# Three blocks of the input projection cut anew, the first one changing from eight products to seven on its way

## The chip, the cores and the metric

The kernel runs on one core of a Trainium2 chip. The metric is the device time of one execution in microseconds (us); smaller is better. A core has TensorE (matrix products), VectorE, ScalarE and GpSimd (element-wise work), and SyncE, whose queue issues all transfers of this kernel. In the profile they are PE (PEld for the loading of weights), DVE, ACT, POOL and SP.

## The reference: what is computed

One layer of a streaming encoder runs for 2048 prompt tokens and 32 sample tokens, which share the weights. The model width is 1024. Only the first step matters here, the combined input projection of the normed tokens:

```python
hp = rmsnorm(xp, g_pre_mix[l])
qa, ka, va, qb, kb, vb, g_low, r = jnp.split(h @ w_in, IN_OFFSETS, axis=-1)
```

`w_in` has 1024 rows and 3088 columns: queries, keys and values of a banded softmax attention (512 columns each), queries and keys (256 each) and values (512) of a gated linear attention (GLA), 16 columns for a forget gate of low rank, and 512 columns `r` for an output gate. Behind it come both attentions, an output projection, cross-attention into 256 memory rows, and a SwiGLU feed-forward of hidden width 2816.

All is in float32, and the kernel gets float32 accuracy out of a faster matmul type: every operand is split into a high part and a low part, and each product is made of three matmuls (high x high, high x low, low x high).

## The kernel before

**Pairs and blocks.** The 2080 tokens are cut into three blocks (`PB`, L604) of 256, 384 and 400 token pairs. A block of h pairs holds 2h neighbouring tokens; its first h tokens are column half c = 0, the other h are c = 1. The 1024 rows of the contraction are halved too (kh = 0 and 1, four tiles of 128 rows each). So the product of a block with 256 columns of `w_in`, which are themselves two halves of 128, is a product of two 2x2 block matrices.

**Eight or seven products.** Multiplied plainly, such a product takes eight half-size products (`fm_eight` L868, and `eight` inside `tm_unit` L920). Block 0 is done so: its moving operands are x times the gain, without the norm, which is multiplied in when a result leaves the accumulator (`r0`, L724). Blocks 1 and 2 use a scheme of the Strassen-Winograd kind with seven products (`fm_unit` L888, `seven` inside `tm_unit`): `seven_mov` (L663) forms sums and differences of the four quarters of x in place and splits seven operands, `seven_sta` (L678) does the same to the weights, and results are combined when they are evicted. With seven products, the norm has to be multiplied into x first (`scale`, L777).

**Units.** A block is worked through in ten units, in this order: a (attention values and the 16 gate columns, token-major, 264 columns to a matmul), two units of queries, two of keys, one of GLA queries, one of GLA keys, two of gates, and v (GLA values, token-major, 256 columns). The eight units between a and v are feature-major: their matmuls have as many columns as the block has pairs. A feature-major unit takes 96 matmuls by eight products and 84 by seven; a token-major one takes 96 or 84 for each 128 tokens of a column half. The last block has 16 tokens over in each half, its tail, with 48 matmuls more in each token-major unit.

**What VectorE does in it.** For a seven-product unit it makes four sums or differences and seven low parts of 512 elements per partition (twice as many of 264 or 256 columns in the token-major units), three of the seven evictions, and for queries and keys two more low parts of the results. For an eight-product unit there are four low parts and no sums. Between blocks it makes the moving operands: four sums and seven low parts of 4h elements. ScalarE makes the high parts.

**Buffers.** The seven moving operands have a buffer each (`mps`, L709); block 0 puts its four operands into the first four (`first_operands`, L808). Seven "stage" buffers (L710) hold raw x, squares and results on their way out; eight buffers hold split weights, four hold raw ones, four hold results that wait to be combined (`cp`). The accumulators have three banks for X, three for Y and Z, and two for small things.

**Order.** Within the program, loads and norms of the next block are woven between the units of the present one (`weave`, L598). The true order of each engine's queue is then made by a planner (`Order`, L49 to 487): it holds a cost for every instruction, plays the whole kernel forward and backward many times with priorities that are partly drawn at random, and fixes the best order it met. Each engine's queue runs in the order fixed there, SyncE's transfers among them. So a change at one place can reorder other places.

**Behind the projection.** Results go to DRAM in pieces by block (`PBLK`, L605) and are read back by the attentions, which begin near 530 us. They cut the tokens by another table (`BLK`).

Of the kernel before, what the change touches and what calls it, by code (L numbers as in the profile page):

```python
# [11 lines left out]
F32R = mybir.dt.float32r  # L12
AF = mybir.ActivationFunctionType
ALU = mybir.AluOpType
# [5 lines left out]
P = 128  # L20
# [4 lines left out]
T = TP + TS  # L25
# [465 lines left out]
def encoder_step(ctx, tc, ins, outs):  # L491
# [27 lines left out]
    gains = {}  # L519
# [81 lines left out]
        return [it for *_, it in sorted(todo, key=lambda x: x[:3])]  # L601


    PB = [(0, 256), (512, 384), (1280, 400)]  # L604
    PBLK = [(s, 2 * h) for s, h in PB]  # L605
    BLK = [(0, 512), (512, 512), (1024, 512), (1536, 544)]
    NB = len(BLK)
# [46 lines left out]
    HK = KT // 2  # L654
# [50 lines left out]
    with ExitStack() as ph:  # L705
        def pool(name, bufs, **kw):
            return ph.enter_context(tc.tile_pool(name=name, bufs=bufs, **RW, **kw))

        mps = [pool(f"pm{i}", 1) for i in range(7)]  # L709
        stp = pool("pst", 7)  # L710
        wp = pool("pw", 8)
        cpp = pool("pc", 4)
# [13 lines left out]
        def stage(name, dt=F32):  # L726
            return stp.tile([P, 1600], dt, tag="stage", name=name)


        def quarters(b, first=False):  # L730

            s, h = PB[b]
            raw, rst = {}, {}

            def load(c, kh):
                r = stage(f"x{b}_{kh}{c}")[:, : HK * h].rearrange("p (k n) -> p k n", k=HK)
                raw[kh, c] = r
                with tc.high_priority(offset=2 * PRI if first else 0):
                    SP.dma_start(r, xt_in[kh * 512 : kh * 512 + 512, s + c * h : s + c * h + h].rearrange("(k p) n -> p k n", p=P))

            def squares(c, kh):
                if first:
                    sq = stage(f"xs{b}_{c}{kh}")[:, : HK * h].rearrange("p (k n) -> p k n", k=HK)
                    ACT.activation(sq, raw[kh, c], AF.Square)
                    add(DVE, sq[:, 0:2], sq[:, 0:2], sq[:, 2:4])
                    if kh == 0:
                        rst["sq", c] = sq
                        return
                    add(DVE, sq[:, 0:2], sq[:, 0:2], rst["sq", c][:, 0:2])
                    rst["sq", c] = sq  # L750
                    return
                if kh == 0:
                    rst[c] = nrm.tile([P, 400], F32, tag="rs", name=f"xr{b}_{c}")[:, :h]
                for kk in range(HK):
                    if kh == 0 and kk == 0:
                        ACT.activation(rst[c], raw[kh, c][:, kk], AF.Square)
                    else:
                        sq = nrm.tile([P, 400], F32, tag="sq", name=f"xs{b}_{c}{kh}{kk}")[:, :h]
                        ACT.activation(sq, raw[kh, c][:, kk], AF.Square)
                        add(POOL, rst[c], rst[c], sq)  # L760

            def rstd(c):
                ps = pt.tile([P, 512], F32, tag="pt", name=f"xn{b}_{c}")
                if first:
                    nt = h // P
                    for kk in range(2):
                        PE.matmul(ps[:, :h], lhsT=ones, rhs=rst["sq", c][:, kk], start=kk == 0, stop=kk == 1)
                    for t in range(nt):
                        for kk in range(2):
                            PE.matmul(ps[:, h + t : h + t + 1], lhsT=rst["sq", c][:, kk, t * P : t * P + P], rhs=ones[:, 0:1], start=kk == 0, stop=kk == 1, skip_group_check=True)  # L770
                    ACT.activation(ps[:, : h + nt], ps[:, : h + nt], AF.Ln, bias=eps_t, scale=1.0 / D)
                    ACT.activation(r0[:, c, : h + nt], ps[:, : h + nt], AF.Exp, scale=-0.5)
                    return
                PE.matmul(ps[:, :h], lhsT=ones, rhs=rst[c], start=True, stop=True)
                rst[c] = rstd_of(ps[:, :h], D)

            def scale(c, kh):  # L777
                for kk in range(HK):
                    v = raw[kh, c][:, kk]
                    DVE.scalar_tensor_tensor(out=v, in0=v, scalar=gains["g_pre_mix"][:, kh * HK + kk : kh * HK + kk + 1], in1=rst[c], op0=ALU.mult, op1=ALU.mult)  # L780

            items = []
            for c in range(2):
                items += [partial(load, c, 0), partial(load, c, 1)]
            for c in range(2):
                items += [partial(squares, c, 0), partial(squares, c, 1), partial(rstd, c)]
                if not first:
                    items += [partial(scale, c, 0), partial(scale, c, 1)]
            return items, raw

        def operands(b, raw):
            h = PB[b][1]
            ops, tail = [], None
            if b == len(PB) - 1:
                tail = kp.tile([P, 2, KT, 32], F32R, tag="tail", name="tail")
                for (kh, c), r in raw.items():
                    t = tail[:, :, kh * HK : kh * HK + HK, c * 16 : c * 16 + 16]
                    split(t[:, 0], t[:, 1], r[:, :, h - 16 : h], DVE)

            def put(v, eng):  # L800
                m_ = mps[len(ops)].tile([P, 2, HK, 400], F32R, tag="mov", name=f"mi{b}_{len(ops)}")
                split(m_[:, 0, :, :h], m_[:, 1, :, :h], v, eng)
                ops.append((m_[:, 0, :, :h], m_[:, 1, :, :h]))

            seven_mov(raw, put)
            return ops, tail
# [80 lines left out]

        def fm_unit(b, ops, col, name):  # L888

            if b == 0:  # L890
                return fm_eight(b, ops, col, name)
            h = PB[b][1]
            w = weights_fm(col, name)
            st = stage(name + "_st")[:, : 4 * h].rearrange("p (a n) -> p a n", a=2)
            dst = {(a, c): st[:, a, c * h : c * h + h] for a in range(2) for c in range(2)}
            cp = [cpp.tile([P, 800], F32, tag="cp", name=f"{name}_c{i}")[:, :h] for i in range(3)]

            def prod(ps, i, first):
                mm3(ps, [((w[i][0][:, k], w[i][1][:, k]), (ops[i][0][:, k], ops[i][1][:, k])) for k in range(HK)], first, True, not first)

            X = px.tile([P, 512], F32, tag="px", name=name + "_X")[:, :h]
            Y = py.tile([P, 512], F32, tag="py", name=name + "_Y")[:, :h]
            Z = py.tile([P, 512], F32, tag="py", name=name + "_Z")[:, :h]
            prod(X, 0, True)
            out(ACT.copy, cp[0], X)
            prod(Y, 1, True)
            out(ACT.copy, cp[1], Y)
            prod(X, 2, False)
            out(ACT.copy, cp[2], X)
            prod(Y, 3, False)  # L910
            out(add, DVE, dst[0, 1], cp[2], Y)
            prod(X, 4, False)
            out(add, DVE, dst[1, 1], cp[1], X)
            prod(Z, 5, True)
            out(add, DVE, dst[0, 0], cp[0], Z)
            prod(X, 6, False)
            out(ACT.copy, dst[1, 0], X)
            return st

        def tm_unit(b, ops, tail, col, low, dst, name):  # L920
# [66 lines left out]
                        for a in range(2):  # L987
                            out(ACT.mul, st[c][:, t, a], banks[a][t], r0[:, c, h + t : h + t + 1])

            T = seven() if b else eight()  # L990
            lt = kp.tile([16, 800], F32, tag="lt", name=name + "_low") if low else None

            def gate(view, n, t0):
# [118 lines left out]

            return [partial(load, 0), partial(load, 1), partial(squares, 0), partial(squares, 1), scale]

        items, raw = quarters(0, True)
        with tc.high_priority(offset=2 * PRI):
            for it, by in zip(items, (0.0, 0.0, 3000.0, 3000.0, 6000.0, 6000.0, 6000.0, 6000.0 + 3000.0, 6000.0 + 3000.0, 6000.0 + 3000.0)):
                with issue_order.shifted(by):
                    it()
        for b in range(len(PB)):  # L1120
            ops, tail = operands(b, raw) if b else first_operands(raw)
            units = [partial(tm_unit, b, ops, tail, 1024, True, vad[b], f"wva{b}")]
            units += [partial(queries, b, ops, u) for u in range(2)] + [partial(keys, b, ops, u) for u in range(2)]
            units += [partial(gla_qk, b, ops, 1536, qbd, 0.125, f"wqb{b}"), partial(gla_qk, b, ops, 1792, kbd, None, f"wkb{b}")]
            units += [partial(gates, b, ops, u) for u in range(2)]
            units += [partial(tm_unit, b, ops, tail, 2048, False, vbd[b], f"wvb{b}")]
            if b == 0:
                units = [units[i] for i in FIRST_ORDER]
            extra = []
            if b == 0:  # L1130
                extra += [partial(load_gain, g) for g in ("g_post_mix", "g_pre_mem", "g_mem", "g_post_mem", "g_pre_ffn", "g_post_ffn")]
            if b == 1:
                extra += [bias_rows] + [partial(bias_copies, h) for h in range(HA)]
            if b + 1 < len(PB):
                items, raw = quarters(b + 1)
                extra += items
            else:
                extra += mem_norm()
            for it in units[:1] + weave(units[1:-1], extra) + units[-1:]:
                it()  # L1140
        SP.dma_start(outs["av_t"], vad[-1][256:])


    DVE.tensor_scalar(out=g16, in0=gains["g_pre_mem"], scalar1=0.0625, scalar2=None, op0=ALU.mult)
# [689 lines left out]
    with ExitStack() as ph:  # L1834
# [255 lines left out]
        late = []  # L2090
# [680 lines left out]
```

## Time and profile before

| What | us |
|---|---|
| Median of three runs | 2903.05 (2900.72 to 2905.3) |
| The profiled execution | 2903.03 |
| Its span in the profile | 2901.2 |
| First matmul of the projection | 7.88 |
| Block 0's last unit ends, block 1 begins | 151.70 |
| Block 1's last unit ends, block 2 begins | 333.9 |
| The projection's last matmuls, memory keys begin | 529.83 |

A row of a group of instructions names the line, the engine, the operation, what is written and read, the shape, the count, then the busy time and the mean duration in ns of one, then the idle time of the engine just before them and what ended it. A line is often that of a helper: L596 is every matmul of the projection and L529 every low part, so tiles are told apart by name: `wva` is a, `wqa`, `wka`, `wqb`, `wkb` and `wr` are queries, keys, GLA queries, GLA keys and gates, `wvb` is v, `mi` a moving operand; `_s` is a split weight, `_st` a result, `_c` one that waits to be combined. A timeline row has the start, the length, and how many instructions were merged into it.

### The profile page before, as it was taken

How to read it: one execution, taken by the hardware profiler on the slowest of the kernel's cores; microseconds unless marked ns; L12 is line 12 of the kernel's file. 1: busy time of each engine (PE TensorE's matmuls, PEld its weight loads, DVE VectorE, ACT ScalarE, POOL GpSimd, SP SyncE). 2: the span in 40 equal slices, each digit the busy share in tenths (PEclk: the TensorE clock that was granted, in tenths of full speed). 3: DMA queues.
4: the chain of work that ended last, by engine and by line, in shares of the span. 5: the costliest groups of instructions: out<-in, count | busy, mean ns of one | idle time of the engine just before them, and what ended most of it. 6: DMA issues, size and time to landing. Idle time of an engine off the chain costs nothing.

```text
span 2901.2 us, 49346 instructions
## 1 busy us (share of the span) xinstructions
PE 2856.5 (98%) x18162; PEld 2442.1 (84%) x18162; DVE 1888.6 (65%) x3366; ACT 1497.7 (52%) x2996; POOL 649.6 (22%) x982
## 2 busy tenths in 40 slices
PE   8999999999999999999999999999999999999998
PEld 8999999887888787987888888887888878777888
DVE  5687976576675667785578766657655556345655
ACT  5556655567786777676546533335433334323333
POOL 0202000367585757000003111113111111000013
PEclk9999999999999999999999999999999999999999
DMA  7656374786586757557567555455543345886665
GB/s 207 198 169 209 118 214 143 240 256 197 175 272 183 230 168 232 176 173 238 185 218 240 181 176 171 151 171 201 168 157 104 119 145 174 284 287 224 204 228 187
DMA packets 463862, 563.90 MB, mean 194 GB/s; under 512 B 55777, under 2 KB 309802, under 8 KB 463586
## 3 DMA queue, kind: packets, MB, share of 16 engines
q1 hardware_dynamic: 463618, 560.73, 60.1%
q8 instruction: 143, 2.34, 0.3%
q14 instruction: 101, 0.83, 0.1%
HBM read 399.75 MB, written 164.02 MB: 194 GB/s over the span
## 4 chain that ended last, share of the span: by engine, by line
PE 58%; DMA 1%; POOL 0%; ACT 0%; DVE 0%; issue 0%; DVEq 0%; ACTq 0%; POOLq 0%
PE pdn L596 13%; PE pg_X L596 8%; PE pu_X L596 8%; PE mops L596 6%; PE pg_Y L596 4%; PE pu_Y L596 4%; PE ms_X L596 3%; PE pg_Z L596 2%; PE pu_Z L596 2%; PE wops L596 2%; PE ms_Y L596 2%; PE ms_Z L596 1%; PE mpt L2007 0%; PE tsgate L2383 0%; PE tsup L2383 0%; PE utp L2592 0%
## 5 line engine op out<-in xcount | busy, mean ns | idle before, releaser
L596 PE MATMUL pdn<-ur,wd_s 128*128 128x512 f32 (+1 forms) x1980 | 431.1, 378 | 4.5 <-ACT ur L533 3.4
L596 PEld LDWEIGHTS pdn<-ur,wd_s 128*128 128x128 f32 x1980 | 354.6, 188 | 77.9 <-ACT ur L533 4.2
L596 PE MATMUL pg_X<-mf,wg_s 128*128 128x512 f32 x1056 | 262.2, 393 | 0.0
L596 PE MATMUL pu_X<-mf,wu_s 128*128 128x512 f32 x1056 | 258.8, 390 | 0.0
L596 PEld LDWEIGHTS pg_X<-mf,wg_s 128*128 128x128 f32 x1056 | 197.4, 188 | 47.4 <-issue 6.0
L596 PEld LDWEIGHTS pu_X<-mf,wu_s 128*128 128x128 f32 x1056 | 198.3, 188 | 42.1
L529 DVE TENSOR_TENSOR wu_s<-wu_r,wu_s 128x512 fp32r<-128x512 f32 x154 | 107.7, 702 | 145.8 <-ACT wu_s L528 141.9
L528 ACT CAST wg_s<-wg_r 128x512 fp32r<-128x512 f32 x154 | 95.4, 621 | 172.9 <-PE pu_X L596 70.5
L596 PE MATMUL mops<-mo,vw 128*128 128x512 f32 x768 | 180.7, 394 | 0.0
L529 DVE TENSOR_TENSOR wg_s<-wg_r,wg_s 128x512 fp32r<-128x512 f32 x154 | 111.7, 727 | 99.3 <-ACT wg_s L528 98.1
L596 PEld LDWEIGHTS mops<-mo,vw 128*128 128x128 f32 x768 | 143.5, 188 | 32.7 <-issue 1.9
L528 ACT CAST wu_s<-wu_r 128x512 fp32r<-128x512 f32 x154 | 95.2, 621 | 142.9 <-PE pg_X L596 51.4
L1570 PE MATMUL wops<-om,wo_s 128*128 128x512 f32 x576 | 154.3, 405 | 1.3 <-POOL om L534 1.0
L534 DVE TENSOR_TENSOR ur<-ur 128x2048 fp32r<-128x2048 f32 (+1 forms) x42 | 90.4, 2154 | 65.2 <-ACT ur L533 65.2
L596 PE MATMUL pg_Y<-mf,wg_s 128*128 128x512 f32 x528 | 130.0, 391 | 0.0
L596 PE MATMUL pu_Y<-mf,wu_s 128*128 128x512 f32 x528 | 129.9, 391 | 0.0
L534 POOL TENSOR_TENSOR mf<-mf 128x512 fp32r<-128x512 f32 x24 | 39.2, 1661 | 402.8 <-DMA hop<-hp 382.1
L1570 PEld LDWEIGHTS wops<-om,wo_s 128*128 128x128 f32 x576 | 104.1, 188 | 24.0 <-POOL om L534 1.7
L533 ACT CAST ur<-ur 128x2048 fp32r<-128x2048 f32 (+1 forms) x42 | 74.1, 1765 | 96.6 <-DMA ur<-ud 96.3
L596 PEld LDWEIGHTS pu_Y<-mf,wu_s 128*128 128x128 f32 x528 | 99.1, 188 | 21.5
L596 PEld LDWEIGHTS pg_Y<-mf,wg_s 128*128 128x128 f32 x528 | 99.0, 188 | 21.4
L1249 PE MATMUL s<-ks,qbuf 128*128 128x256 f32 (+2 forms) x448 | 112.7, 342 | 4.3 <-DVE u_mn L1224 3.9
(606 smaller groups left out, 6535.1 us busy)
## 6 DMA issues: line engine op xcount, KB each, us to landing
ud<-u SPq DMA_DIRECT2D x154, 256.0 KB, 3.8
ur<-ud SPq DMA_DIRECT2D x28, 1024.0 KB, 6.7
wg_r<-in_w_ffn_gate_dram SPq DMA_DIRECT2D x44, 512.0 KB, 3.8
wu_r<-in_w_ffn_up_dram SPq DMA_DIRECT2D x44, 512.0 KB, 5.5
wd<-in_w_dn_dram SPq DMA_DIRECT2D x72, 256.0 KB, 4.7
wo_r<-in_w_o_dram SPq DMA_DIRECT2D x64, 256.0 KB, 3.9
mf<-hop SPq DMA_DIRECT2D x14, 1024.0 KB, 7.4
wdr<-in_w_dn_dram SPq DMA_DIRECT2D x22, 512.0 KB, 6.2
```

The costliest lines, as they stand in the source:

```text
L528: ACT.copy(hi, src)
L529: (lo_eng or DVE).tensor_tensor(out=lo, in0=src, in1=hi.bitcast(F32), op=ALU.subtract)
L533: ACT.copy(m[:, 0], m[:, 1].bitcast(F32))
L534: (POOL if on_pool else DVE).tensor_tensor(out=m[:, 1], in0=m[:, 1].bitcast(F32), in1=m[:, 0].bitcast(F32), op=ALU.subtract)
L596: PE.matmul(ps, lhsT=a, rhs=b, start=first and i == 0, stop=last and i == len(seq) - 1, skip_group_check=skip)
L1249: PE.matmul(ps_out, lhsT=q[:, 2 * i + e, q0 : q0 + nq], rhs=ks[:, e, k0 : k0 + ncol], start=i == 0, stop=i == 1)
L1570: PE.matmul(ps, lhsT=a, rhs=b, start=i == 0, stop=i == len(seq) - 1)
```

## The change

The blocks become 384, 384 and 272 pairs. Block 0 begins with eight products as before, but only for its first three units (a and both query units, `EIGHT = 3`). Then a step `late` multiplies gain and norm into the raw x of block 0, which is kept until then, and makes the seven operands; keys, GLA, gates and v of block 0 go by seven products. The seven operands of every block get their buffers in another order (`HOME`), so that the first three don't lie in those that the eight products read. Block 2, now the narrowest, goes by seven products as before.

```diff
-    PB = [(0, 256), (512, 384), (1280, 400)]
+    PB = [(0, 384), (768, 384), (1536, 272)]
...
-        mps = [pool(f"pm{i}", 1) for i in range(7)]
+        HOME = (4, 5, 6, 0, 1, 2, 3)
+        mps = {i: pool(f"pm{i}", 1) for i in HOME}
...
+        EIGHT = 3
...
             def scale(c, kh):
+                r = r0[:, c, :h] if first else rst[c]
                 for kk in range(HK):
                     v = raw[kh, c][:, kk]
-                    DVE.scalar_tensor_tensor(out=v, in0=v, scalar=gains["g_pre_mix"][:, kh * HK + kk : kh * HK + kk + 1], in1=rst[c], op0=ALU.mult, op1=ALU.mult)
+                    DVE.scalar_tensor_tensor(out=v, in0=v, scalar=gains["g_pre_mix"][:, kh * HK + kk : kh * HK + kk + 1], in1=r, op0=ALU.mult, op1=ALU.mult)
...
-                m_ = mps[len(ops)].tile([P, 2, HK, 400], F32R, tag="mov", name=f"mi{b}_{len(ops)}")
+                m_ = mps[HOME[len(ops)]].tile([P, 2, HK, 400], F32R, tag="mov", name=f"mi{b}_{len(ops)}")
...
-            if b == 0:
+            if type(ops) is dict:
                 return fm_eight(b, ops, col, name)
...
-            T = seven() if b else eight()
+            T = eight() if type(ops) is dict else seven()
...
+            def late():
+                nonlocal ops
+                for it in scales:
+                    it()
+                ops, _ = operands(0, raw0)
...
             if b == 0:
                 units = [units[i] for i in FIRST_ORDER]
+                raw0 = raw
+                units[EIGHT - 1 : EIGHT] = [units[EIGHT - 1], late]
...
-        SP.dma_start(outs["av_t"], vad[-1][256:])
+        SP.dma_start(outs["av_t"], vad[-1][PBLK[-1][1] - 544 :])
```

The last line only follows the new cut: the same rows are copied out.

More of the change, by code (lines that the diff above doesn't have):

```diff
@@ L788, in quarters @@
                     items += [partial(scale, c, 0), partial(scale, c, 1)]
-            return items, raw
+            return items, raw, [partial(scale, c, kh) for c in range(2) for kh in range(2)]
         def operands(b, raw):
@@ L1113, in mem_norm @@
             return [partial(load, 0), partial(load, 1), partial(squares, 0), partial(squares, 1), scale]
-        items, raw = quarters(0, True)
+        items, raw, scales = quarters(0, True)
         with tc.high_priority(offset=2 * PRI):
@@ L1120, in encoder_step, with unit @@
         for b in range(len(PB)):
[L1121 to L1126, printed above, removed]
+            if b == 0:
+                ops, tail = first_operands(raw)
+            else:
+                ops, tail = operands(b, raw)
+            def unit(f, *a):
+                return lambda: f(a[0], ops, *a[1:])
+            def late():
[3 more added lines that the diff above has]
+                ops, _ = operands(0, raw0)
+            units = [unit(tm_unit, b, tail, 1024, True, vad[b], f"wva{b}")]
+            units += [unit(queries, b, u) for u in range(2)] + [unit(keys, b, u) for u in range(2)]
+            units += [unit(gla_qk, b, 1536, qbd, 0.125, f"wqb{b}"), unit(gla_qk, b, 1792, kbd, None, f"wkb{b}")]
+            units += [unit(gates, b, u) for u in range(2)]
+            units += [unit(tm_unit, b, tail, 2048, False, vbd[b], f"wvb{b}")]
             if b == 0:
                 units = [units[i] for i in FIRST_ORDER]
+                raw0 = raw
+                units[EIGHT - 1 : EIGHT] = [units[EIGHT - 1], late]
             extra = []
@@ L1134, in encoder_step @@
             if b + 1 < len(PB):
-                items, raw = quarters(b + 1)
+                items, raw, _ = quarters(b + 1)
                 extra += items
```

## The prediction

> **What bounds the kernel now.** I read the page first (shares and slices), then the table of stretches cut at the units of the projection, TensorE's timeline for the price of one matmul of each width, VectorE's groups by form, and the list of TensorE's waits.
>
> ```profile
> span 2901.2 us, 49346 instructions
> PE 2856.5 (98%) x18162; PEld 2442.1 (84%) x18162; DVE 1888.6 (65%) x3366; ACT 1497.7 (52%) x2996; POOL 649.6 (22%) x982
> PE wva_X L596 <- ACT wva_s L528: 7.9, 1, 7.9
> PE wqa_X L596 <- ACT wqa_c L700: 1.7, 1, 1.7
> ```
>
> TensorE is busy for 98% of the span. In the projection (0 to 530 us) it waits twice: 7.9 us before the first matmul and 1.7 us in the first query unit of block 1. So a microsecond of matmuls taken out is a microsecond of time, as long as the other engines keep up. VectorE is the next engine: it prepares the moving operands, the weights and a part of the evictions. The table of stretches gives length, then TensorE, weight loads, VectorE, ScalarE, GpSimd busy, clock, DMA share and GB/s. A stretch is one or two units: v of block 0; a of block 1; first queries of block 1; v of block 1; a of block 2; then queries, keys, the two GLA units and gates of block 2.
>
> ```profile
> 129.00:151.70 22.70, 22.70 (x195) 22.70 (x194) 18.15 (x20) 14.65 (x21) 0.00 (x0) 1.00 0.32 103
> 151.70:182.30 30.60, 30.60 (x255) 30.58 (x254) 26.73 (x41) 16.39 (x31) 0.00 (x0) 1.00 0.38 123
> 182.30:212.00 29.70, 27.98 (x162) 27.27 (x161) 20.32 (x31) 14.86 (x31) 0.00 (x0) 1.00 0.78 233
> 304.05:333.90 29.85, 29.85 (x253) 29.85 (x253) 26.54 (x39) 22.14 (x36) 0.00 (x0) 1.00 0.38 126
> 333.90:370.50 36.60, 36.60 (x306) 35.92 (x304) 31.59 (x44) 18.23 (x37) 0.00 (x0) 1.00 0.36 119
> 370.50:401.80 31.30, 31.30 (x175) 30.82 (x173) 22.53 (x34) 16.66 (x34) 0.00 (x0) 1.00 0.73 227
> 401.80:432.40 30.60, 30.60 (x171) 30.60 (x170) 22.15 (x33) 16.23 (x27) 0.00 (x0) 1.00 0.81 244
> 432.40:462.70 30.30, 30.30 (x168) 30.30 (x167) 21.53 (x32) 16.49 (x27) 0.00 (x0) 1.00 0.54 169
> 462.70:494.20 31.50, 31.50 (x175) 31.39 (x173) 20.62 (x34) 16.33 (x28) 0.00 (x0) 1.00 0.34 117
> ```
>
> From v of block 1 to the gates of block 2 TensorE never waits, and VectorE works 145.0 of 190.2 us, 76%. Its fullest row, 333.90 to 370.50, stands at 86%.
>
> **The change: matmuls.** The price of one is the distance between the starts of two rows, divided by the matmuls between them (the records of a few are missing, so I count them from the code).
>
> ```profile
> 60.15 1.57 PE L596 MATMUL wka_X<-mi,wka_s 128*128 128x256 f32 x12
> 82.64 1.46 PE L596 MATMUL wqb_X<-mi,wqb_s 128*128 128x256 f32 x11
> ...
> 151.70 4.53 PE L596 MATMUL wva_X<-wva_s,mi 128*128 128x264 f32 x36
> 156.06 4.40 PE L596 MATMUL wva_Y<-wva_s,mi 128*128 128x264 f32 x35
> ...
> 214.39 2.26 PE L596 MATMUL wka_X<-mi,wka_s 128*128 128x384 f32 x12
> 243.77 2.26 PE L596 MATMUL wqb_X<-mi,wqb_s 128*128 128x384 f32 x12
> ...
> 304.05 4.44 PE L596 MATMUL wvb_X<-wvb_s,mi 128*128 128x256 f32 x36
> 308.32 4.31 PE L596 MATMUL wvb_Y<-wvb_s,mi 128*128 128x256 f32 x35
> ...
> 401.83 2.34 PE L596 MATMUL wka_X<-mi,wka_s 128*128 128x400 f32 x12
> 432.37 2.16 PE L596 MATMUL wqb_X<-mi,wqb_s 128*128 128x400 f32 x11
> ```
>
> Two key units of eight products are 192 matmuls in 22.49 us: 117.1 ns at 256 columns. Two of seven products are 168: 29.38 us is 174.9 ns at 384, 30.54 us is 181.8 ns at 400. The token-major ones cost 4.36/36 = 121.1 ns at 264 and 4.27/36 = 118.6 ns at 256. Between 256 and 384 a column costs 0.45 ns, so 272 columns are 117.1 + 16 x 0.45 = 124.3 ns (estimate).
>
> A feature-major unit has 96 matmuls by eight products, 84 by seven; there are eight such units. Before: 768 x 117.1 + 672 x 174.9 + 672 x 181.8 ns = 89.9 + 117.5 + 122.2 = 329.6 us. After: block 0 has 2 x 96 + 6 x 84 = 696 of 384 columns, 121.7 us; block 1 is as it was, 117.5; block 2 has 672 of 272, 83.5; together 322.7. That is 6.9 us less. The a unit goes from 192 + 252 + 252 = 696 to 288 + 252 + 168 = 708 matmuls (its tail stays): 12 x 121.1 ns = 1.5 us more. The v unit goes from 696 to 252 + 252 + 168 = 672: 24 x 118.6 ns = 2.8 us less. Sum: 8.2 us less.
>
> Block 0's norm grows with its width.
>
> ```profile
> 7.88 0.81 PE L596 MATMUL wva_X<-wva_s,mi 128*128 128x264 f32 x2 [7.88 <-ACT wva_s L528]
> ...
> 27.73 1.03 PE L767 MATMUL xn<-xs,ones 128*128 128x256 f32 x4
> 28.60 0.95 PE L770 MATMUL xn<-ones,xs 128*128 128x1 f32 x8
> 29.41 1.11 PE L767 MATMUL xn<-xs,ones 128*128 128x256 f32 x4
> ```
>
> The wide part takes 0.87 us per column half, the per-token part 0.81; each becomes 1.5 times as long, for two halves 2 x 0.5 x 1.68 = 1.7 us more. Block 2's norm shrinks by some 0.2. TensorE's sum: 8.2 - 1.5 = 6.7 us less.
>
> **The start.** The first load of x grows from 512 to 768 KB, the squares and the first operands by half.
>
> ```profile
> 0.74 0.44 SPq L739 DMA_DIRECT2D x<-in_x_t_dram  x1
> ...
> 4.56 1.06 ACT L744 ACTIVATE xs<-x 128x1024 f32<-128x1024 f32 x1 [2.54 <-DMA x<-in_x_t_dram]
> ```
>
> The load takes 3.8 us to its first use; half of that again, 1.9, is the upper end, none the lower; I take 0.9, since part of it is latency. The squares add 0.5. Against it, 144 matmuls lie between 7.88 and 27.73, 17.4 us of work in 19.8: the ramp loses 2.4 us because operands come slowly, and operands that feed three token tiles in place of two starve it less; 0.5 back. Net 1 us later, between 0 and 3.
>
> **VectorE's share, on which the sign hangs.**
>
> ```profile
> L529 DVE TENSOR_TENSOR wka_s<-wka_r,wka_s 128x512 fp32r<-128x512 f32 x7 | 4.8, 692 | 1.9 <-ACT wka_s L528 1.7
> L529 DVE TENSOR_TENSOR kl<-wka_st,kh 128x800 fp32r<-128x800 f32 x3 | 3.0, 990 | 0.3 <-ACT kh L528 0.3
> L529 DVE TENSOR_TENSOR kl<-wka_st,kh 128x768 fp32r<-128x768 f32 x4 | 3.8, 954 | 0.2
> L661 DVE TENSOR_TENSOR wka_st<-wka_c,wka_X 128x400 f32<-128x400 f32 x2 | 1.1, 572 | 1.7 <-PE wka_X L596 1.7
> L661 DVE TENSOR_TENSOR wva_st<-wva_c,wva_X 128x264 f32<-128x264 f32 x3 | 1.2, 423 | 0.0
> L529 DVE TENSOR_TENSOR wva_s<-wva_r,wva_s 128x528 fp32r<-128x528 f32 x11 | 7.3, 703 | 0.0
> L529 DVE TENSOR_TENSOR mi<-x,mi 128x1600 fp32r<-128x1600 f32 x7 | 12.8, 1822 | 0.7 <-ACT mi L528 0.7
> L529 DVE TENSOR_TENSOR mi<-x,mi 128x1536 fp32r<-128x1536 f32 x7 | 12.3, 1756 | 3.8 <-ACT mi L528 3.7
> L780 DVE SCALAR_TENSOR_TENSOR x<-x,g_pre_mix,xn 128x384 f32<-128x384 f32 x16 | 9.1, 608 | 0.5 <-ACT xn L539 0.5
> ```
>
> The weights of a seven-product unit cost VectorE 4 sums and 7 low parts of 512 elements whatever the block's width: 11 x 0.692 = 7.6 us, a sum taken like a low part. A key unit adds 3 evictions and 2 low parts. At 400 that is 7.6 + 3 x 0.57 + 2 x 0.99 = 11.3 us (the stretch shows 22.15 / 2 = 11.1) beside 15.3 us of matmuls. At 272 it is 7.6 + 3 x 0.43 + 2 x 0.71 = 10.3 us (0.43 and 0.71 off the slopes between the rows) beside 84 x 0.1243 = 10.4. Before, the narrow block was the one with eight products, whose four low parts cost VectorE 2.8 us.
>
> From v of block 1 to the gates of block 2, after: v 22 x 0.69 + 9 x 0.42 = 19.0; block 2's operands, 11 operations of 1088 at 1.756 - 448 x 0.00103 = 1.29 us, 14.2; a 24 x 0.703 + 6 x 0.42 = 19.4; four query and key units 41.2; two gate units the same, 20.6; two GLA units without low parts 17.8; the memory rows' norm (3 sums and 8 scalings of 128x256 to 128x1024) some 5.5 by the 692 ns row. Together 137.7 us. TensorE has there 252 x 0.1186 + 216 x 0.1211 + 83.5 = 139.6. VectorE would be at 99% where it was at 76%. It can't be: a low part waits for ScalarE's high part, the next sum in place waits for both (the first row: 1.9 us lost in the seven low parts it groups), and VectorE's queue runs in order. At an efficiency of 95% the stretch takes 137.7 / 0.95 = 144.9, 5.3 us over; the weights prepared ahead (8 buffers) absorb some 1.3 of it; I take 4. The ends are 0 (every gap filled) and 13.4 (90%, 153.0 us).
>
> The same at the seam of blocks 0 and 1: v 19.0, operands 11 x 1.756 = 19.3, a 22 x 0.703 + 9 x 0.42 = 19.2, together 57.5 beside 29.9 + 30.5 = 60.4 us, 95%; before, 44.9 of 53.3, 84%. I take 1 us, between 0 and 3. The 1.7 us wait in the first queries stays: that unit is unchanged.
>
> Costed at nothing: block 0's late scaling and operands (16 scalings of 0.61 and 11 operations of 1.76, 29 us of VectorE). They go between first operands and keys, beside some 68 us of matmuls (288 x 0.121 + 192 x 0.175) in which VectorE has about 34 us of other work (first operands, squares, a's eight low parts, two query units, the first key weights). The seven homes are ordered so that the first three operands need no buffer of the eight products. DMA: a query unit of block 2 moves 2.7 MB (1.0 of weights, 1.7 stored) in 10.4 us, 257 GB/s; the keys' row above shows 244 at a share of 0.81, so the queue holds, narrowly. Later stages read the same bytes in as many pieces; their order is planned anew, which I bound at 3 us either way.
>
> **Sum.** The profiled execution took 2903.03 us (median of the runs 2903.05). -6.7 + 1 + 4 + 1 = -0.7: 2902.3 us, no change. About 0.2%, 5.8 us, is what a measurement can tell from none. The forecast's own range is 2898 to 2908.
>
> [...]
>
> **Rivals.** (1) Full cover: the planner fills VectorE's gaps, and only TensorE's sum and the start count: 2903.0 - 6.7 + 1 = 2897.3; if the 1.7 us wait goes too, 2895.6. For it: 145.0 us of VectorE work never made TensorE wait there. Against it: the load has never been near 99%. (2) VectorE bounds block 2, slower: at 90% the stretch costs 13.4 us and the seam 3, so 2903.0 - 6.7 + 1 + 16.4 = 2913.7. It decides below about 92%. For it: the fullest whole row is 86%. (3) The late operands of block 0 come late: four are written into the buffers of the eight products, and the last can start only when those end; uncovered, two operands and two sums at 1.76 us with ScalarE's parts are some 6 us: 2908. For it: the place is new. Against it: the last product comes six products (12.6 us) after the first.
>
> **Chances.** Forecast 0.40, full cover 0.32 (0.22 beyond the bound, 0.10 within), VectorE-bound 0.20, late operands 0.08 (half beyond). So faster 0.22, within 0.54, slower 0.24. The range runs from full cover with a lucky order to the VectorE-bound case: 2893.5 to 2914.
>
> **What would show it.** A matmul of 272 columns at 124 ns; the first matmul near 9 us; VectorE over 93% from v of block 1 to the gates of block 2, with waits of TensorE there on low parts (L529) or evictions of 1 to 10 us in sum; no wait between block 0's queries and keys. Wrong: no such waits (then 2897), waits over 10 us, or a 272-column matmul bound by its weight load at over 130 ns.

## The result and the profile after

| | before | after |
|---|---|---|
| Median of six executions each, in us | 2900.82 (2897.35 to 2905.3) | 2890.56 (2887.87 to 2894.75) |
| Ratio, with its 95% interval | | 0.9963 [0.9952, 0.9974] |
| The profiled execution | 2903.03 | 2889.52 |
| First matmul of the projection | 7.88 | 8.53 |
| Memory keys begin (the projection's end) | 529.83 | 525.35 |
| From there to the first gate matmul of the feed-forward | 1042.4 | 1037.0 |

The kernel became faster by 10.3 us, and the forecast of 2902.3 with its range from 2893.5 missed it. The two profiled executions lie 13.5 us apart: 4.5 in the projection, 5.4 between it and the feed-forward, 3.6 in the feed-forward and down projection.

First two lines of the page of the changed kernel:

```profile
span 2887.7 us, 49361 instructions
PE 2842.6 (98%) x18086; PEld 2430.7 (84%) x18086; DVE 1948.4 (67%) x3446; ACT 1524.9 (53%) x3051; POOL 650.2 (23%) x982
```

TensorE has 76 matmuls fewer on record and is busy 13.9 us less; VectorE has 80 instructions and 60 us more. TensorE's waits in the projection of the changed kernel (total, times, longest):

```profile
PE wva_X L596 <- ACT wva_s L528: 8.5, 1, 8.5
PE wvb_Z L596 <- ACT wvb_s L528: 1.5, 1, 1.5
...
PE wvb_X L596 <- ACT wvb_s L528: 0.4, 1, 0.4
PE wvb_T L596 <- DVE wvb_s L529: 0.4, 1, 0.4
```

The 1.7 us wait in the first queries of block 1 is gone; new are 2.3 us in the last unit, v of block 2. TensorE's timeline of the changed kernel gives the prices:

```profile
8.53 1.03 PE L596 MATMUL wva_X<-wva_s,mi 128*128 128x264 f32 x3 [8.53 <-ACT wva_s L528]
...
28.11 1.45 PE L770 MATMUL xn<-xs,ones 128*128 128x384 f32 x4
33.29 1.71 PE L596 MATMUL wva_X<-wva_s,mi 128*128 128x264 f32 x12
...
432.82 1.67 PE L596 MATMUL wka_X<-mi,wka_s 128*128 128x272 f32 x12
447.89 1.67 PE L596 MATMUL wka_Y<-mi,wka_s 128*128 128x272 f32 x12
```

The norm takes 33.29 - 28.11 = 5.2 us (3.4 before, 27.73 to 31.16). Between the two key rows lie ten products of 12 matmuls: 15.07 / 120 = 125.6 ns for 272 columns.

The table of stretches of the changed kernel, columns as before: the seam of blocks 0 and 1; v of block 1 to the gates of block 2; the first key unit and more of block 2; v of block 2; and all between the projection and the feed-forward.

```profile
174.79:235.20 60.41, 60.41 (x506) 60.39 (x506) 52.54 (x74) 36.94 (x62) 0.00 (x0) 1.00 0.42 133
354.57:497.00 142.43, 141.90 (x1146) 140.38 (x1146) 125.06 (x207) 90.40 (x179) 0.00 (x0) 1.00 0.61 196
432.82:452.40 19.58, 19.58 (x158) 19.58 (x157) 16.80 (x29) 10.81 (x22) 0.00 (x0) 1.00 0.88 287
497.00:525.40 28.40, 26.51 (x224) 25.63 (x222) 19.67 (x35) 16.02 (x33) 0.00 (x0) 1.00 0.48 142
525.40:1562.40 1037.00, 1011.34 (x8213) 848.38 (x8213) 728.49 (x1702) 699.66 (x1679) 439.18 (x827) 0.99 0.69 216
```

The last stretch in the kernel before:

```profile
529.83:1572.20 1042.37, 1018.27 (x8216) 851.90 (x8214) 720.61 (x1699) 696.27 (x1676) 436.23 (x825) 0.99 0.68 213
```

VectorE is busy for 125.06 of 142.43 us, 88% and not over 93%, and TensorE runs on. Behind the projection both kernels issue the same matmuls, yet TensorE is busy 7 us less.

So two questions go to the experiments. Why didn't VectorE bound the projection? And is the time behind the projection a matter of the order that the planner happened to come to (theory A), or do the new cuts shorten those stages themselves, through the pieces in which results are stored and read back (theory B)?

### The profile page after: what moved, and what is told of

It is laid out like the page before. It is cut to its first block, busy times and chain, and to the rows that moved or that the text cites. A ratio compares the mean times of both kernels' runs of the same rounds, so it can differ in the third digit from the quotient of the medians.

```text
span 2887.7 us, 49361 instructions
## 1 busy us (share of the span) xinstructions
PE 2842.6 (98%) x18086; PEld 2430.7 (84%) x18086; DVE 1948.4 (67%) x3446; ACT 1524.9 (53%) x3051; POOL 650.2 (23%) x982
## 3 DMA queue, kind: packets, MB, share of 16 engines
q8 instruction: 142, 2.33, 0.3%
## 4 chain that ended last, share of the span: by engine, by line
PE 91%; DMA 3%; POOL 2%; DVE 2%; ACT 1%; issue 1%; SPq 0%; DVEq 0%; POOLq 0%; ACTq 0%
PE pdn L596 14%; PE pg_X L596 8%; PE pu_X L596 8%; PE mops L596 6%; PE wops L1588 5%; PE pg_Y L596 4%; PE pu_Y L596 4%; PE ms_X L596 3%; PE pg_Z L596 2%; PE pu_Z L596 2%; PE po L1273 2%; PE s L1267 2%; PE wva_X L596 2%; PE pt L1296 2%; PE wka_X L596 2%; PE wqa_X L596 2%
```

## The experiments: each half of the change alone

**Only the cuts.** Block 0 has 384 pairs, but goes by eight products throughout.

```diff
-                units[EIGHT - 1 : EIGHT] = [units[EIGHT - 1], late]
```

> The new cuts with all of block 0 by eight products: no late operands. By the matmul prices, block 0 has 8 x 96 matmuls of 384 columns in place of 696 (72 x 174.9 ns = 12.6 us more than the changed kernel) and a v unit of 288 in place of 252 (36 x 118.6 ns = 4.3 us more), so the projection ends near 525.4 + 16.9 - 2 = 540 (the late waits in v may go). Theory A: nothing of the gain is left, 8 to 14 us slower than the kernel before, whatever the later order does beyond some us. Theory B: the later stages keep their 9 us, and it is within 4 us of the kernel before.

Measured: 2920.14 us, ratio 1.0063 [1.0048, 1.0078]; the projection ends at 545.3. TensorE's wait on the combined results in it:

```profile
PE wqa_X L596 <- ACT wqa_c L700: 1.7, 1, 1.7
```

Twelve matmuls more in each of six units and 36 in v are 72 x 0.1749 + 36 x 0.1186 = 16.9 us; the projection is 19.9 longer than the changed kernel's. TensorE's waits behind its first matmul make 1.7 of the rest: 4.1 us here (this wait, 1.3 before the memory keys, 1.0 in v and gates) against 2.4 there. Some 1.2 us more of busy time is not accounted for.

**Only the late switch.** The old cuts, but block 0 (256 pairs) goes over to seven products behind its third unit.

```diff
-    PB = [(0, 384), (768, 384), (1536, 272)]
+    PB = [(0, 256), (512, 384), (1280, 400)]
```

> The old cuts of 256, 384, 400 with the change to seven products after three units. By the matmul prices block 0 saves 72 matmuls of 256 columns and 24 of v, 8.4 + 2.8 = 11.3 us, more than the new cuts with it (8.2). If VectorE is no bound, the projection ends near 529.8 - 11.3 = 518.5. If VectorE bounds a narrow block, block 0's key and gate units, 10.2 us of VectorE work beside 9.8 us of matmuls with the late operands ahead of them, make TensorE wait by 3 to 8 us, and it ends at 522 to 526.

Measured: 2912.34 us, ratio 1.0034 [1.0022, 1.0046]; the projection ends at 538.3, where the matmuls alone would give 518.5. The first two rows are block 0 after the switch and its seam to block 1, the last two are a part of the first:

```profile
76.00:106.00 30.00, 24.71 (x172) 23.29 (x173) 29.76 (x39) 19.93 (x42) 18.19 (x14) 0.89 0.72 234
156.00:180.00 24.00, 22.61 (x172) 21.16 (x172) 23.79 (x27) 16.00 (x29) 0.00 (x0) 1.00 0.28 92
98.00:102.00 4.00, 1.67 (x14) 1.47 (x13) 4.00 (x6) 1.42 (x3) 3.77 (x4) 1.00 0.58 151
102.00:106.00 4.00, 4.00 (x23) 4.00 (x23) 3.96 (x9) 1.48 (x3) 0.27 (x1) 0.58 0.54 150
```

VectorE is busy for 99% of both rows and TensorE stands in between, 5.3 us in the first row and 1.4 in the second: the VectorE bound of rival 2 exists, with short units of 256 columns and the late operands on top. But in the first row VectorE is also slow. Two of its low parts of one shape, and GpSimd beside the second:

```profile
78.22 0.69 DVE L529 TENSOR_TENSOR wqb_s<-wqb_r,wqb_s 128x512 fp32r<-128x512 f32 x1
82.40 1.50 DVE L529 TENSOR_TENSOR wqb_s<-wqb_r,wqb_s 128x512 fp32r<-128x512 f32 x1
```

```profile
79.28 12.71 POOL L661 TENSOR_TENSOR xr<-xr,xs 128x384 f32<-128x384 f32 x9 [78.84 <-ACT xs L762]
```

From 79.7 to 89.5 us, while GpSimd sums the squares of block 1, VectorE's operations of 512 elements take 1.38 to 1.50 us in place of 0.69, and TensorE's waits of 0.70, 0.61 and 1.65 us fall there. The changed kernel does these sums from 101.7 to 129.9 us, has slow operations there too (`kl` of 768 elements 1768 ns, `ql` of the same shape 950) and doesn't wait. So how much of the first row is VectorE's plain load, and how much this slowing, was not separated; the second row, with GpSimd idle, is the load alone.

A row further shows the second cost: after 4 us in which TensorE works only 1.67, its clock is at 0.58. Waits (9.4 us more than before) and clock (3.3) make 12.7 of the 19.8 us lost; the rest stands in TensorE's busy time. So each half alone loses, and only together do they gain: behind the wide block's units TensorE doesn't wait for the late operands.

## The experiments: VectorE in block 2

**More work for VectorE.** Three of seven low parts of each feature-major unit of block 2 are computed twice.

```diff
+                    if b == 2 and len(ops) in (2, 4, 6):
+                        hi, lo = ops[-1]
+                        DVE.tensor_tensor(out=lo, in0=raw[q], in1=hi.bitcast(F32), op=ALU.subtract)
```

> The changed kernel, in whose block 2 three of the seven low parts of each feature-major unit are computed twice with the same result: 24 x 0.69 = 16.6 us more of VectorE, nothing else. From v of block 1 to the end of the gates VectorE was busy 125.1 of 142.4 us. If it can be filled to 98.5%, as a narrow block 0 showed, it takes in some 15 us and TensorE waits 2 to 4 us more: the projection ends at 527 to 530. By the 95% of the prediction it takes in 10 us, and the projection ends at 532 or later.

Measured, in one execution: 2896.8 us (before beside it 2901.72); the projection ends at 528.0. Two stretches of it, the whole from v of block 1 on and the fullest part:

```profile
453.00:476.00 23.00, 22.58 (x177) 22.04 (x176) 22.54 (x40) 14.79 (x28) 0.00 (x0) 1.00 0.73 220
354.60:528.00 173.40, 170.53 (x1366) 166.63 (x1365) 160.53 (x265) 106.66 (x213) 0.35 (x2) 1.00 0.59 184
```

With 24 operations more, VectorE is at 98% in the part, TensorE still at 98% there, and the projection ends only 2.6 us later than the changed kernel's. (With its instructions unchanged, that kernel's projection ends between 521.9 and 527.4 in five orders, further down: differences of 2 or 3 us between single runs may be the order's.) An efficiency of 95% is no limit.

**Less work for VectorE.** One of the four sums of each block 2 unit goes to GpSimd.

```diff
-                seven_sta([raw], lambda q: ops.append(wsplit(raw[q], f"{name}_s{len(ops)}")))
+                seven_sta([raw], lambda q: ops.append(wsplit(raw[q], f"{name}_s{len(ops)}")), POOL if b == 2 else None)
...
-                seven_sta(raws, put)
+                seven_sta(raws, put, POOL if b == 2 else None)
```

> The changed kernel, in whose block 2 one of the four sums of each weight unit goes from VectorE to GpSimd, which is idle there: 8 x 0.69 + 4 x 0.70 = 8.3 us less of VectorE. If VectorE's backlog makes the 2.3 us of waits in v of block 2, they go, and the projection ends near 523; if those waits come from the chain of one unit's own high and low parts, they stay or grow, since GpSimd's sum takes longer, and it ends at 525 to 527.

Measured: 2891.86 us, ratio 0.9971 [0.9961, 0.9980]; the projection ends at 523.5. The largest waits of TensorE near it:

```profile
PE w_mkps L1588 <- DVE w_mkf L1705: 1.5, 1, 1.5
PE w_mkps L1588 <- ACT mm L533: 1.4, 1, 1.4
```

None is left in v, and the projection is 1.9 us shorter. That doesn't show that VectorE's backlog made the 2.3 us there. From 354.6 us to the projection's end VectorE is busy for 143.1 us in place of 144.7: of the 8.3 us taken off, most came back in other operations that took longer (`kl` of 544 elements 889 ns, 718 in the changed kernel). And the changed kernel has an order in which nothing waits in v though VectorE does all its work itself (new_order_5 below; from 354.6 us on and v alone):

```profile
354.60:521.90 167.30, 167.10 (x1359) 165.08 (x1358) 144.24 (x238) 106.00 (x210) 2.63 (x13) 1.00 0.60 194
497.00:521.90 24.90, 24.90 (x213) 24.48 (x212) 19.33 (x34) 15.05 (x32) 2.63 (x13) 1.00 0.58 177
```

So VectorE's load costs this projection from nothing to some 2 us, by the order that the planner came to.

## The experiments: where the switch stands, and the homes

**Switch after the first unit.**

```diff
-        EIGHT = 3
+        EIGHT = 1
```

> The changed kernel with only the a unit of block 0 by eight products. Matmuls: two query units of 84 in place of 96, 24 x 174.9 ns = 4.2 us less. VectorE theory: the late operands (29 us) now lie beside the a unit alone; VectorE has 10 us of first operands, 4.5 of squares, 5.6 of a's low parts, 29 and 7.6 of the first query weights, 57 us, before TensorE's 42 us of a and norm have ended, so TensorE waits about 10 us before or in the first queries: the projection ends near 525.4 - 4.2 + 10 = 531. If the late operands are no bound: 521 and no wait at the queries.

Measured: 2900.67 us, ratio 0.9997 [0.9987, 1.0007]; the projection ends at 528.2. The stretches around the switch and the wait in them:

```profile
52.00:62.00 10.00, 6.92 (x35) 5.81 (x34) 9.90 (x12) 6.73 (x15) 0.00 (x0) 0.92 0.28 77
56.00:60.00 4.00, 1.15 (x4) 0.57 (x4) 3.97 (x6) 2.96 (x6) 0.00 (x0) 1.00 0.30 41
60.00:64.00 4.00, 4.00 (x13) 3.55 (x14) 3.97 (x5) 1.38 (x3) 0.00 (x0) 0.57 0.30 115
```

```profile
PE wqa_Z L596 <- ACT wqa_s L528: 2.2, 1, 2.2
```

It saves 24 matmuls of 174.9 ns, 4.2 us, and ends 2.9 us later: 7.1 us lost. Three waits at the switch (2.19, 0.59 and 0.29 us) are 3.1 of them, and the clock behind them 1.7, as above; another 1.7 is the clock in v of block 2 (0.57 from 511 to 515 us), where the changed kernel has nearly the same waits and keeps it. VectorE is at 99% at the switch, with GpSimd idle. Behind three units the same operands cost nothing.

**The homes in plain order.**

```diff
-        HOME = (4, 5, 6, 0, 1, 2, 3)
+        HOME = (0, 1, 2, 3, 4, 5, 6)
```

> The changed kernel with the seven operands in the buffers 0 to 6 in order, so that the first four wait for the eight products of the second query unit to end. Buffer theory: VectorE can't begin the operands before half of that unit is done, and needs 19 us for them beside 8 us of query matmuls and 12.6 us of key products, with 12 us of its own other work: TensorE waits 4 to 10 us in the first keys, the projection ends at 529 to 535. If the order of the buffers doesn't matter: 525.4 within 1 us.

Measured: 2895.72 us, ratio 0.9978 [0.9965, 0.9991]; the projection ends at 527.9. The stretch where the keys of block 0 follow the late operands:

```profile
85.00:105.00 20.00, 20.00 (x116) 20.00 (x115) 19.05 (x23) 13.73 (x25) 4.99 (x5) 1.00 0.81 250
```

TensorE doesn't wait; the planner interleaved the two key units. Its projection is 2.6 us longer than the changed kernel's. Of these 1.7 are the clock, at 0.58 from 510 to 514 us behind 2.5 us of waits in v of block 2, as other orders have them, and 0.9 are waits: rival 3's buffers cost nothing that these runs can tell.

## The experiments: the order alone

The planner's settings are changed and nothing else; the instructions stay the same. Each kernel was given new orders with such an edit (the seed is in `Random`, L459):

```diff
-    PASSES, DRAWS, SPREAD = 9, 50, 200.0
+    PASSES, DRAWS, SPREAD = 3, 50, 200.0
```

With seed 2, the planner came to the changed kernel's very order again, so that this run is a repeat of it: the same order was 10.3 us faster than the kernel before in one set of executions and 6.5 in the other. The expectations in the order in which they were written; in the last four, theories A and B are put to the test by means.

> The kernel before with only the planner's random draws changed; every instruction stays, only orders differ. Theory A (of the 10.3 us gained only 4.5 come from the projection, the rest from an order of the later stages that the planner happened to draw): the projection ends within 1 us of 529.8, and the stretch behind it, 2371 us in the kernel before, moves by 3 to 10 us either way. Theory B (the new cuts themselves make the later stages shorter): that stretch stays within 3 us of 2371.

> The changed kernel with only the planner's draws changed. Theory A: the projection ends near 525.4, within 1.5 us, and the stretch behind it, 2362 us in the changed kernel, moves by 3 to 10 us, so that the gain over the kernel before can be anything from 0 to 12 us. Theory B: the stretch stays at 2362, and the whole gain of some 10 us stays.

> The changed kernel with six passes of the planner in place of nine, which gives TensorE another order; the instructions are the same. Theory A (what is gained behind the projection depends on the order that the planner came to): the projection ends within 1.5 us of 525.4, and the stretch from there to the first gate matmul of the feed-forward, 1037.0 us in the changed kernel and 1042.4 before, moves by 3 us or more, most likely up. Theory B (the new cuts make the attention stage shorter): it stays within 2 us of 1037.

> The changed kernel with three passes of the planner: a third order of the same instructions. From the projection's end to the first gate matmul of the feed-forward the changed kernel took 1037.0 us, a repeat of it 1035.8, its other order 1040.0; the kernel before 1042.4 and in another order 1044.9. Theory A (that stretch depends on the order the planner came to, and old and new cuts draw from the same spread): between 1038 and 1048. Theory B (the new cuts shorten it by 5 us): between 1035 and 1040.

> The kernel before with draws three times as wide: a third order of the same instructions. Theory A: the same stretch lies anywhere from 1036 to 1048. Theory B: it stays between 1042 and 1046.

> The kernel before with three passes of the planner, a fourth order. Theory A: the stretch lies anywhere from 1036 to 1050. Theory B: between 1042 and 1046.

> The changed kernel in another order of its own (PASSES 7). Its projection should end near 525 by both theories. Theory A (behind the projection only the order that the planner happened to come to counts): the stretch from the end of the projection to the first gate matmul of the feed-forward lies anywhere between 1031 and 1045 us, its mean of 1041 being likeliest, the time then 2894 to 2900. Theory B (the new cuts themselves make the later stages 6 us shorter, as the means of 1036 for the three orders of the changed kernel and 1042 for the four of the kernel before would have it): the stretch is 1031 to 1038, the time 2888 to 2893.

> The changed kernel in a fifth order (PASSES 3, seed 2). As for the fourth: projection ends near 525; by theory A a stretch between 1031 and 1045 with 1041 likeliest, by theory B between 1031 and 1038. Both theories are judged by the mean of the five orders of the changed kernel against the six of the kernel before: under 3 us apart for A, 5 to 7 us apart for B.

> The kernel before in a fifth order (PASSES 3, seed 2). The projection should end near 529. Theory A: the stretch behind it lies anywhere between 1031 and 1045, so that one of the new orders of the kernel before may well come below 1038, and the time then below 2897. Theory B: 1038 to 1045 as in its four other orders, the time 2898 to 2904.

> The kernel before in a sixth order (PASSES 3, seed 3). As for the fifth: projection near 529; by theory A a stretch anywhere between 1031 and 1045, by theory B 1038 to 1045 and a time of 2898 to 2904.

The stretch is that from the projection's end to the first gate matmul. TensorE's idle time in it is the length less its busy time; the time lost to the clock is length x (1 - granted clock), summed over 26 equal parts of the stretch.

| Kernel and order | Median | Ratio [95%] | Projection ends | Stretch | Idle | Lost to the clock |
|---|---|---|---|---|---|---|
| before, as given | 2900.82 | | 529.8 | 1042.4 | 24 | 14 |
| before, seed 2 | 2900.71 | 0.9999 [0.9990, 1.0008] | 531.4 | 1044.9 | 25 | 13 |
| before, spread 600 (before_replan) | 2901.56 | 0.9999 [0.9990, 1.0008] | 527.8 | 1038.3 | 25 | 9 |
| before, 3 passes (before_replan_2) | 2902.07 | 1.0002 [0.9993, 1.0011] | 527.9 | 1044.0 | 26 | 12 |
| before, 3 passes, seed 2 (old_order_5) | 2900.46 | 1.0001 [0.9989, 1.0012] | 528.3 | 1040.1 | 22 | 16 |
| before, 3 passes, seed 3 (old_order_6) | 2900.1 | 1.0001 [0.9992, 1.0011] | 529.2 | 1040.7 | 26 | 12 |
| after, as given | 2890.56 | 0.9963 [0.9952, 0.9974] | 525.4 | 1037.0 | 26 | 12 |
| the same order once more (after_draw2) | 2894.06 | 0.9978 [0.9968, 0.9987] | 525.4 | 1035.8 | 26 | 9 |
| after, 6 passes (after_replan) | 2895.97 | 0.9986 [0.9974, 0.9997] | 527.4 | 1040.0 | 28 | 10 |
| after, 3 passes (after_replan_2) | 2887.87 | 0.9957 [0.9942, 0.9973] | 522.6 | 1031.5 | 23 | 9 |
| after, 7 passes (new_order_4) | 2894.8 | 0.9984 [0.9974, 0.9994] | 525.0 | 1041.5 | 28 | 12 |
| after, 3 passes, seed 2 (new_order_5) | 2904.71 | 1.0016 [1.0004, 1.0028] | 521.9 | 1055.9 | 27 | 26 |

**The projection** ends at 527.8 to 531.4 in six orders with the old cuts (mean 529.1) and at 521.9 to 527.4 in five with the new ones (mean 524.5). The two don't overlap, if only by 0.3 us: 4.6 us is the change's own.

**Behind it** the means are 1041.7 and 1041.2 us, 0.5 apart, where theory B asked for 5 to 7 and theory A for less than 3. By that it falls, but five orders are few: the changed kernel's spread over 24 us, and without new_order_5 their mean is 1037.5, 4.2 less than before. A share of some us of the new cuts themselves is neither shown nor excluded. What is shown is how much the changed kernel's order decides: the same instructions take 1031.5 us in one order and 1055.9 in another, and with that one the whole kernel is slower than before although its projection is the shortest of all. Of the 24 us, 21 show in the last two columns: 4 us of idle time and 17 of lost clock.

First starts in the fifth order of the changed kernel, then in its third, from the rows of two tiles (shortest, median and longest of one in ns; first and last start):

```profile
L1588 PE MATMUL w_mkps<-mm,w_mk_s x192: 274/281/582, 521.9 to 576.1; 128*128 128x256 f32 x192
L596 PE MATMUL pg_X<-mf,wg_s x1056: 387/389/798, 1577.8 to 2429.1; 128*128 128x512 f32 x176
```

```profile
L1588 PE MATMUL w_mkps<-mm,w_mk_s x192: 274/282/579, 522.6 to 573.5; 128*128 128x256 f32 x192
L596 PE MATMUL pg_X<-mf,wg_s x1056: 387/389/798, 1554.1 to 2405.0; 128*128 128x512 f32 x176
```

How the clock is lost, in the fifth order of the changed kernel: stretches of 4 us in the attentions, and TensorE's timeline there.

```profile
976.00:980.00 4.00, 3.58 (x45) 2.72 (x45) 1.21 (x6) 2.70 (x8) 4.00 (x5) 1.00 0.96 307
980.00:984.00 4.00, 2.38 (x12) 1.66 (x12) 0.00 (x0) 3.62 (x12) 4.00 (x5) 0.76 0.81 247
984.00:988.00 4.00, 3.61 (x12) 2.30 (x11) 2.16 (x4) 2.85 (x9) 3.84 (x8) 0.50 0.58 200
988.00:992.00 4.00, 4.00 (x17) 3.72 (x16) 0.69 (x1) 1.56 (x5) 2.33 (x8) 0.50 0.84 268
992.00:996.00 4.00, 4.00 (x18) 2.69 (x18) 0.59 (x1) 2.11 (x5) 2.56 (x10) 0.50 0.26 77
996.00:1000.00 4.00, 4.00 (x45) 3.81 (x43) 2.05 (x6) 2.42 (x7) 3.59 (x4) 0.61 0.18 68
```

```profile
980.52 0.55 PE L1296 MATMUL pt<-ident,u_sb 128*128 128x128 f32 x3 [0.90 <-ACT prt L1298]
980.90 0.38 PE L1284 MATMUL po<-ident,inv 128*128 128x128 f32 x2
982.39 3.38 PE L1296 MATMUL pt<-ident,u_sb 128*128 128x128 f32 x12 [1.11 <-ACT prt L1298]
...
988.40 1.70 PE L1677 MATMUL rt<-ones,acc 128*128 128x1 f32 x8
```

Two waits of 0.90 and 1.11 us, 0.8 us of matmuls between them, and the clock stands at half for the next 17 us. The waits cost 2 us, the clock (0.24 + 3 x 0.50 + 0.39) x 4 = 8.5.

Waits close together do not always cost the clock. In v of block 2 the changed kernel as given has two, 1.50 and 0.39 us, its order of 6 passes has 1.58 and 0.39, at the same place. The stretch with these waits and the one behind it, in the first, then in the second:

```profile
506.00:510.00 4.00, 2.11 (x17) 1.54 (x16) 3.40 (x6) 3.97 (x9) 0.00 (x0) 1.00 0.02 6
509.00:513.00 4.00, 4.00 (x37) 3.94 (x36) 2.27 (x4) 3.85 (x10) 0.00 (x0) 1.00 0.38 117
```

```profile
505.00:509.00 4.00, 2.25 (x17) 1.76 (x16) 3.72 (x7) 3.46 (x7) 0.00 (x0) 1.00 0.30 87
509.00:513.00 4.00, 3.78 (x20) 3.35 (x21) 2.41 (x5) 3.97 (x10) 0.00 (x0) 0.57 0.25 85
```

The first keeps the clock, the second loses 1.7 us by it. In the stretch behind the projection of the kernel before and of the changed kernel as given, the clock is at 0.50 for 3.41 us at a time or for 6.83 (in the changed one from 565.79 to 569.20 and from 541.89 to 548.72 us, for example), which costs 1.7 or 3.4 us. What decides whether two such waits cost it was not shown: no run moved the waits alone.

## Why the prediction was wrong, step by step

**TensorE's sum held.** 272 columns cost 125.6 ns for 124.3, the norm 1.75 us more for 1.7; TensorE's busy time up to the projection's end fell from 520.2 to 514.4 us, by 5.8, where 6.7 were forecast; the 1.3 ns times 672 matmuls are these 0.9 us. **The start** moved by 0.65 us, for 1 forecast.

**The failed step of the first half: "VectorE would be at 99% ... It can't be."** The count was good. Counts times means of VectorE's groups between 354.57 and 497.00 add up to 136.9 us, against 137.7; at the seam to 57.7 against 57.5. But the engine is busy for 125.1 and 52.5 us. The sum of durations isn't the time that the engine needed: its operations overlapped. The kernel before showed it already, in VectorE's timeline (start, length; each row ends with the number of operations merged in it):

```profile
145.53 1.32 DVE L529 TENSOR_TENSOR wva_s<-wva_r,wva_s 128x528 fp32r<-128x528 f32 x2
146.76 1.32 DVE L658 TENSOR_TENSOR wva_r<-wva_r 128x528 f32<-128x528 f32 x2
148.00 1.32 DVE L661 TENSOR_TENSOR wva_r<-wva_r,wva_r 128x528 f32<-128x528 f32 x2
149.24 1.75 DVE L529 TENSOR_TENSOR mi<-x,mi 128x1536 fp32r<-128x1536 f32 x1
```

Six operations of 703 ns take 149.24 - 145.53 = 3.71 us, 0.62 each. So the prediction set a sum of durations (99%) beside a busy share (76%), which are unlike: as sums, the kernel before has 153.0 of 190.2 us, 80%. With VectorE given still more, 175.4 us of durations went into 173.4 (vector_more), for 2.6 us. Thus 4 us forecast for block 2 were 2.3 in the order as given, all in its last unit, and none in new_order_5, and 1 for the seam was none. Part of the match between 137.7 and 136.9 is luck: of v's operations 14 were done before the stretch (9.6 us), while its rows hold eight scalings of x (3.9) and five operations of block 2's v (3.4) that the account had not.

**"The 1.7 us wait in the first queries stays: that unit is unchanged"**: it went. In the kernel before it is 1.9 us with seed 2, 0.6 in before_replan, 0.4 in old_order_5 and gone in before_replan_2 and old_order_6, so the order made it, not the unit. From the forecast of -0.7 for the projection: +0.9 for TensorE, -0.4 for the start, -1.7 and -1 for VectorE, -1.7 for this wait make -4.6; measured -4.5. That is rival 1, full cover, in its second form (2895.6). The forecast also started from 2903.03, one execution, where the median of six is 2900.82; 2.2 of the 11.7 us by which it missed lie there.

**The failed step of the second half: "their order is planned anew, which I bound at 3 us either way."** One order of the changed kernel against the first of the kernel before gave 5.4 us there, and its five orders span 24, so 3 us was no bound. Over the five orders the mean ratio is 0.9983 (the first with the mean of its two sets), 5 us, which is about the projection's share. So some 5 of the 10 us are luck, as far as five orders tell: a good order, and a good set of six executions of it. (What the feed-forward gave, 3.6 us between the first two profiles, stays open in part: from its first matmul to the span's end it takes 1325.1 to 1331.9 us in the six orders of the kernel before, 1325.2 to 1326.3 in the five of the changed one. The lowest agree, the means are 2.6 apart, and each is one profiled execution.)

**What was costed at nothing** stayed so: no wait in block 0's keys, none for a transfer at a DMA share of 0.88 in block 2's. The late operands aren't free as such: eight_one shows the price where their cover is thinner, and late_only does with GpSimd's work on top.

**Open:** why the clock stays low for 17 us in one place (new_order_5) and some 3.4 in another (eight_one, 0.57 from 60 to 64 us). What runs there differs: behind eight_one's waits the matmuls have 384 columns each, in new_order_5 there are transposes, eight matmuls of one column and other short ones, which a busy share near 1 doesn't tell apart. The planner reckons with a lower clock too (`WINDOW`, `LITTLE`, `FULL`, L63, used at L395). Whether its numbers fit was not tested, and new_order_5 is an order that it chose. Open is also why VectorE's operations took longer while GpSimd worked (1.38 to 1.50 us in place of 0.69 in late_only), and whether the new cuts gain anything behind the projection. The best order measured is the changed kernel with 3 passes, 2887.87 us.

## What to carry to other kernels

Compare an engine's load by one measure: busy time of a stretch against busy time, or spacing between starts, never durations added up against a busy share. When a change makes a planner draw a new order, the difference of two kernels is that of two draws: give both several orders before a few us are put down to the change or to one edit in it, and look at the part that it touches by itself. Short waits of TensorE close together can cost more in clock than in waiting (8.5 us beside 2 in new_order_5). Before a full VectorE is blamed on its load, see whether its operations became longer, and what GpSimd does then.

## What the runs showed of the hardware

The clock went down to half after short waits: 0.50 after waits of 0.90 and 1.11 us within 4 us (new_order_5), 0.58 after one of 2.33 (late_only), 0.57 after 2.19 and 0.59 (eight_one). The 1.7 us wait of the kernel before left it at 1.00 (194 to 202 us), but the same wait in another order of that kernel, 1.91 us long, took the clock to half (0.57 from 196 to 200 us, before_draw2), and two waits close together kept it in one order and lost it in another (505 to 513 us, above). One row at full clock is no safety.

VectorE's operations of 512 elements took 1.38 to 1.50 us while GpSimd worked and 0.69 when it did not (late_only, 78 to 92 us).
